# Scores of two heads issued in turn into pairs of PSUM banks, and the bias table built in the first projection

## The chip, the cores and the metric

The kernel runs on one core of a Trainium2 chip, in one launch. The metric is the device time of that launch in microseconds (us). TensorE multiplies matrices into PSUM (eight banks of 128 partitions x 512 float32), VectorE and ScalarE (ACT) read PSUM and write SBUF, GpSimd (POOL) works on SBUF and issues small loads, and SyncE (SP) issues the loads of weights.

## The reference

Two layers over 256 tokens of width 1024, all in float32. Each layer has a mixer of three attention branches that share one input projection, and a squared-ReLU MLP.

```python
h = rms_norm(x, norm_mix_pre[l])
dq, dk, dv, mq, mk, mv, c_q, c_kv, k_pe, g = split(h @ w_in[l])
# differential: 4 heads, each with two halves of 64 features
w  = softmax(q1 k1^T/8 + bias) - lam * softmax(q2 k2^T/8 + bias)
oa = rms_norm(w @ v, diff_subln[l]) * (1 - lam_init)
# block attention: 4 heads of 128; one block holds the whole sequence, so it is causal attention
ob = softmax(q k^T * 128**-0.5 + bias) @ v
# latent: 8 heads, 64 features and 32 with rotary positions; values of 64
oc = softmax(q k^T * 96**-0.5) @ v
x  = x + rms_norm(sum(sigmoid(g) * (o @ w_branch)) @ w_out, norm_mix_post[l])
x  = x + rms_norm(relu(rms_norm(x) @ w_up)**2 @ w_down, norm_mlp_post[l])
```

`bias` comes from a table of 32 buckets by 8 heads, looked up by the distance between query and key (T5 buckets); keys behind the query's place are masked.

## The kernel before

Instructions are written in program order with tiles and pools. A planner then fixes the order of each engine's instructions before the run: it takes what is ready by its own estimate of times, and of several ready ones the one that is first in program order. On the chip each engine follows that order and waits at an instruction whose inputs are late.

Weights are float32 and split exactly into two parts (`hi` by ACT at L129, `lo` by VectorE at L130); each product of a projection is three TensorE passes (L176 to L178). Weights are loaded by SP (L137), 512 KB at a time, into five buffers; the split parts have six buffers each.

A layer's mixer runs, in program order: the projection of the latents (`pc`, two token tiles); their norms (`rr`, `cr` are powers on POOL at L117; `cn`, `rope` read `pc`); values and queries and keys of the differential heads (`dv`, `dqk`); in layer 0 the bias table, `lam` and the rotary factors; the differential heads; the same for the block heads (`mv`, `mqk`); the latent heads; then gates (`pg`), the products of the branches (`pb`) and the output projection (`po`). The planner fills TensorE's time between steps of attention with `pmv`, `pmqk` and `pg` products.

A head's scores are two float32 products, 128 queries x 128 keys (L354) and 128 queries x 256 keys (L355), each of which the chip runs as two passes. `softmax` adds the bias (VectorE, L345) and takes the exponent (ACT, L348). Probabilities are transposed on TensorE (L361), copied by ACT (L363, `pt`) and multiplied with the values (L374 and L375 for block and latent heads, L500 to L502 for differential ones). A differential head uses the scores' banks again: `pss[0]` for its output, `pss[1]` for the transposed output (L516).

PSUM: the pool `p_acc` has four single banks, `p_mm` two, `p_tr` two. `p_acc` holds the scores, `pc`, `pcols` (rows of norm weights brought onto partitions), `pb`, and the accumulators of the output projection and of the MLP's second product (four at once).

The bias table is built by `setup_bias`: two small loads on POOL (`oh`, `tab`), one product (`pbias`, L266), a copy into a staging tile `cb` (L270), a write to scratch memory in HBM (L272), and a load of 1152 KB that spreads it over 128 partitions (L274). `cb`, `oh` and the tiles `cn`, `lamv`, `lamp` share the three buffers of the pool `prep`.

Of the kernel before, what the change touches and what calls it, by code (L numbers as in the profile page):

```python
# [30 lines left out]
# First relative distance of each T5 bucket that distances 0..255 can reach.  # L31
# [4 lines left out]
def trunk(ctx: ExitStack, tc: tile.TileContext, x, positions, rel_bias, norm_mix_pre, norm_mix_post,  # L36
# [15 lines left out]
    p_acc = ctx.enter_context(tc.tile_pool(name="pacc", bufs=4, space=PSUM))  # L52
# [18 lines left out]
    def acc_tile(name):  # L71
        return p_acc.tile([128, 512], F32, tag="acc", name=name)
# [11 lines left out]
    # Rows of vectors that act on features once those lie on partitions.  # L84
# [26 lines left out]
    def setup_cols(rows, at, n):  # L111
        p = acc_tile("pcols")
        nc.tensor.transpose(p[:, :n], rows[:], ident[:n, :n])
        nc.vector.tensor_copy(cols[:, at:at + n], p[:, :n])
# [17 lines left out]
    def chunk(src, nk, c, name, parts=None, spare=None, quick=False):  # L132
        """One load of weights and its two parts; `spare` is a pool that is idle now."""
        n = nk * c
        raw = raws.tile([128, 1024], F32, tag="raw", name=f"raw_{name}")
        rv = raw[:, :n].rearrange("p (k c) -> p k c", k=nk)
        nc.sync.dma_start(rv, src)  # L137
        if spare is None:
            hi = whi.tile([128, 1024], F32R, tag="hi", name=f"hi_{name}")
            lo = wlo.tile([128, 1024], F32R, tag="lo", name=f"lo_{name}")  # L140
        else:
            pool, tag = spare
            hi = pool.tile([128, 1024], F32R, tag=tag, name=f"hi_{name}")
            lo = pool.tile([128, 1024], F32R, tag=tag, name=f"lo_{name}")
        if parts is None:
            split(hi[:, :n], lo[:, :n], raw[:, :n], quick)
        else:
            at = 0
            for v in parts(raw):
                m = v.shape[1] * v.shape[2]  # L150
                o = [t[:, at:at + m].rearrange("p (a b) -> p a b", a=v.shape[1]) for t in (hi, lo)]
                split(o[0], o[1], v)
                at += m
        return [(hi[:, k * c:(k + 1) * c], lo[:, k * c:(k + 1) * c]) for k in range(nk)]
# [4 lines left out]
    def load_t(w2d, c0, c, name, kts=KT):  # L159
        """Weights that move: kts tiles of [128, c]."""  # L160
        nk = 1024 // c
        r = []
        for k0 in range(0, kts, nk):
            r += chunk(wslice(w2d, k0, nk, c0, c), nk, c, f"{name}_{k0}")
        return r

    def load_f(w2d, c0, name, kts=KT):
        """Weights that stay: two blocks of 128 columns, kts tiles each."""
        r = []
        for k0 in range(0, kts, 4):  # L170
            r += chunk(wslice(w2d, k0, 4, c0, 256), 4, 256, f"{name}_{k0}")
        return [[(h[:, b * 128:(b + 1) * 128], l[:, b * 128:(b + 1) * 128]) for h, l in r] for b in range(2)]
# [58 lines left out]
    def post_norm(xt, ps2, wpost, eps_col):  # L231
        """x += rms_norm(ps2) * wpost"""
        parts = small_tile("pnp", 2)
        yw = slab_tile([128, D], "yw")
        def weigh(h):
            nc.vector.tensor_tensor(yw[:, h * 512:(h + 1) * 512], ps2[h][:],
                                    wpost[:, h * 512:(h + 1) * 512], op=OP.mult)
        for h in range(2):
            nc.scalar.activation(junk, ps2[h][:], AF.Square, scale=1.0 / 32.0, accum_out=parts[:, h:h + 1])
            if h == 0:  # L240
                weigh(0)
        v = small_tile("pnv", 1)
        nc.vector.tensor_scalar(v, parts[:, 0:1], parts[:, 1:2], EPS if eps_col is None else eps_col,
                                op0=OP.add, op1=OP.add)
        q = small_tile("pnq", 1)
        rpow(q, v, 1)
        weigh(1)
        for h in range(2):
            s = slice(h * 512, (h + 1) * 512)
            nc.vector.scalar_tensor_tensor(xt[:, s], yw[:, s], q[:, 0:1], xt[:, s],  # L250
                                           op0=OP.mult, op1=OP.add)

# [24 lines left out]
    def setup_rope():  # L277
# [14 lines left out]
        # Index 0: sine.  Index 1: cosine, the sine a quarter turn on.  # L292
# [24 lines left out]
    def setup_lam():  # L317
# [10 lines left out]
        for l in range(DEPTH):  # L328
            li = 0.8 - 0.6 * math.exp(-0.3 * l)
            nc.vector.tensor_scalar(lam[:, l:l + 1], dots[:, 2 * l:2 * l + 1], dots[:, 2 * l + 1:2 * l + 2], li,  # L330
                                    op0=OP.subtract, op1=OP.add)
            # The weights come out of the chip negated: the sign goes here.
            nc.vector.tensor_scalar(subc[:, l:l + 1], cols[:, 38 + l:39 + l], -(1.0 - li), None, op0=OP.mult)

# [1 line left out]
    last_exp = [None]  # L336

    def softmax(ps, brow):
        e = work_tile("e", "e", 384, 6)
# [12 lines left out]
    def scores(q, k):  # L352
        ps = acc_tile("sc")
        nc.tensor.matmul(ps[:, 0:128], q[:, 0:128], k[:, 0:128], start=True, stop=True)  # L354
        nc.tensor.matmul(ps[:, 128:384], q[:, 128:256], k, start=True, stop=True)  # L355
        return ps

    def transpose_p(p):
        ps = tr_tile("ppt")
        for j in range(3):  # L360
            nc.tensor.transpose(ps[:, j * 128:(j + 1) * 128], p[:, j * 128:(j + 1) * 128], ident[:])  # L361
        pt = work_tile("pt", "pt", 384, 2)
        nc.scalar.activation(pt, ps[:, :384], AF.Copy)  # L363
        return pt
# [7 lines left out]
    def av_f(ps, pt, v0, v1):  # L372
        """ps [c, 256 queries] = v^T p^T"""
        nc.tensor.matmul(ps, v0, pt[:, 0:256], start=True, stop=False)  # L374
        nc.tensor.matmul(ps[:, 128:256], v1, pt[:, 256:384], start=False, stop=True)  # L375

# [7 lines left out]
    def mixer(l, xs, tiles, wc, before):  # L384
# [7 lines left out]
        # latent queries, keys and the shared rope key, token-major  # L392
        wc = wc or load_c(l, 0, 4)
        pcs = []
        for t in range(2):
            pc = acc_tile("pc")
# [3 lines left out]
        if l == 0:  # L400
            more_rows()
            setup_cols(rows1, 16, n_rows - 16)
        rpow(rr, ms, 2)
# [21 lines left out]
        # 1/rms of every token along the free axis, on all partitions  # L425
# [26 lines left out]
        # transposed latents  # L452
# [16 lines left out]
        if l == 0:  # L469
            setup_bias()  # L470
# [4 lines left out]
        # differential attention  # L475
        o_a = []
        for p in range(2):
            ot = out_r(f"oa{p}")
            o_a.append(ot)
            for hh in range(2):  # L480
                h = 2 * p + hh
                es, pss = [], []
                for c in range(2):
                    ps = scores(dqk[p][c * 64:(c + 1) * 64, 0, hh, :], dqk[p][c * 64:(c + 1) * 64, 1, hh, :])
                    pss.append(ps)
                    es.append(softmax(ps, h))
                (e1, s1), (e2, s2) = es
# [34 lines left out]
        # block attention: one block holds the whole sequence, so each query sees its own block  # L522
# [3 lines left out]
        for p in range(2):  # L526
            ot = out_r(f"ob{p}")
            o_b.append(ot)
            for hh in range(2):
                h = 2 * p + hh  # L530
                ps = scores(mqk[p][:, 0, hh, :], mqk[p][:, 1, hh, :])
# [4 lines left out]
                av_f(ps[:, :256], pt, mv[:, 0, vs], mv[:, 1, vs])  # L536
                split_out(ot, hh, ps)

        # latent attention
# [49 lines left out]
        for p in range(2):  # L589
# [21 lines left out]
            for hh in range(2):  # L611
                hs = []
                for par in range(2):
                    qk = lqk[p, par]
                    ps = scores(qk[0:96, 0, hh, :], qk[0:96, 1, hh, :])
                    e, sm = softmax(ps, 8)
                    normalize_p(e, sm)
                    hs.append((4 * p + 2 * hh + par, ps, e))
                po = hs[0][1]
                for par, (h, _, e) in enumerate(hs):  # L620
                    pt = transpose_p(e)
                    vs = slice(h * 64, (h + 1) * 64)
                    av_f(po[par * 64:(par + 1) * 64, :256], pt, vl[:, 0, vs], vl[:, 1, vs])
# [3 lines left out]
        # gates and the products of the three branches, two feature blocks at a time  # L627
# [15 lines left out]
        for d in range(4):  # L643
            m = None
            for b in range(3):
# [3 lines left out]
                pb = acc_tile("pb")  # L649
# [12 lines left out]
        # output projection  # L662
# [15 lines left out]
    def finish(accs, held, xs, wpost, eps_cols, nxt, wcol, stored=None):  # L678
        """The last rows of a projection, the first half of the tokens ahead, and the norm that follows."""
# [15 lines left out]
    def out_proj(l, w2d, act, wpost, xs):  # L695
        """x += rms_norm(mixed @ w_out); the next block's input follows each half of the tokens."""
        tiles = new_act("h2")
        accs = [[acc_tile(f"po{t}{h}") for h in range(2)] for t in range(2)]
# [13 lines left out]
    def mlp(l, xs, tiles, before):  # L712
# [46 lines left out]
        def down(g):  # L759
            if not accs:  # L760
                accs.extend([acc_tile(f"pd{t}{h}") for h in range(2)] for t in range(2))
# [79 lines left out]
```

## Time and profile before

| | us |
|---|---|
| runs | 873.63, 875.62, 876.04 |
| median | 875.62 |
| span of the profiled execution | 874.3 |
| TensorE busy in it | 858.1 |
| VectorE, ACT, POOL busy in it | 539.6, 468.9, 107.1 |

The span goes from the first to the last instruction of one profiled execution; this execution's whole time is not listed apart from it. Busy times overlap. TensorE's passes are pipelined, and the profile models their ends, so that the time that a pass costs is read from its start to the start of the next one. A granted clock of 1.00 is 2.4 GHz, and 0.50 is 1.2 GHz.

### The profile page before, as it was taken

How to read it: one execution, taken by the hardware profiler on the slowest of the kernel's cores; microseconds unless marked ns; L12 is line 12 of the kernel's file. 1: busy time of each engine (PE TensorE's matmuls, PEld its weight loads, DVE VectorE, ACT ScalarE, POOL GpSimd, SP SyncE). 2: the span in 40 equal slices, each digit the busy share in tenths (PEclk: the TensorE clock that was granted, in tenths of full speed). 3: DMA queues.
4: the chain of work that ended last, by engine and by line, in shares of the span. 5: the costliest groups of instructions: out<-in, count | busy, mean ns of one | idle time of the engine just before them, and what ended most of it. 6: DMA issues, size and time to landing. Idle time of an engine off the chain costs nothing.

```text
span 874.3 us, 14960 instructions
## 1 busy us (share of the span) xinstructions
PE 858.1 (98%) x5820; PEld 791.0 (90%) x5820; DVE 539.6 (62%) x921; ACT 468.9 (54%) x820; POOL 107.1 (12%) x130
## 2 busy tenths in 40 slices
PE   7999999999999999999999999999999999999997
PEld 6988999899988999999899899999998899999995
DVE  6757688457867445446575768954578754554452
ACT  6536675644546444445464757664544664444441
POOL 2211210001311000000100012000033010000010
PEclk9999999999999999999999999999999999999999
DMA  8865544356666656667738553546558466665631
GB/s 275 260 168 180 144 124 134 107 178 184 203 232 195 185 182 189 191 193 212 228 97 248 146 149 97 150 117 189 177 187 270 145 218 191 192 193 182 186 115 49
DMA packets 109798, 154.27 MB, mean 176 GB/s; under 512 B 5103, under 2 KB 89136, under 8 KB 109728
## 3 DMA queue, kind: packets, MB, share of 16 engines
q1 hardware_dynamic: 108448, 149.70, 56.4%
q10 hardware_dynamic: 608, 2.11, 0.7%
q0 software_dynamic: 672, 1.51, 0.6%
q8 instruction: 46, 0.75, 0.4%
q14 instruction: 24, 0.20, 0.1%
HBM read 151.19 MB, written 2.11 MB: 175 GB/s over the span
## 4 chain that ended last, share of the span: by engine, by line
PE 88%; issue 4%; DMA 3%; DVE 2%; ACT 1%; POOL 1%; SPq 0%; POOLq 0%; DVEq 0%; ACTq 0%
PE pu L176 7%; PE pu L178 7%; PE pu L177 7%; PE pd L177 6%; PE pd L178 6%; PE pd L176 6%; PE pg L176 5%; PE pg L177 5%; PE pg L178 5%; PE pb L178 3%; PE pb L177 3%; PE pb L176 3%; PE pmqk L178 2%; PE pmqk L177 2%; PE pmqk L176 2%
## 5 line engine op out<-in xcount | busy, mean ns | idle before, releaser
L177 PE MATMUL pu<-h,hi_up 128*128 128x256 f32 x448 | 126.9, 283 | 0.0
L178 PE MATMUL pu<-h,lo_up 128*128 128x256 f32 x448 | 126.8, 283 | 0.0
L176 PE MATMUL pu<-h,hi_up 128*128 128x256 f32 x448 | 126.7, 283 | 0.0
L130 DVE TENSOR_TENSOR lo_wd<-raw_wd,hi_wd 128x1024 fp32r<-128x1024 f32 x64 | 77.7, 1225 | 74.5 <-ACT hi_wd L129 74.5
L129 ACT ACTIVATE hi_wd<-raw_wd 128x1024 fp32r<-128x1024 f32 x64 | 67.0, 1058 | 82.6 <-PE pu L177 38.0
L176 PE MATMUL pg<-h,hi_g 128*128 128x256 f32 x384 | 110.6, 288 | 0.4 <-ACT lqk L602 0.4
L178 PE MATMUL pg<-h,lo_g 128*128 128x256 f32 x384 | 109.7, 286 | 0.0
L177 PE MATMUL pg<-h,hi_g 128*128 128x256 f32 x384 | 109.1, 284 | 0.0
L130 DVE TENSOR_TENSOR lo_up<-raw_up,hi_up 128x1024 fp32r<-128x1024 f32 x64 | 80.2, 1258 | 38.8 <-ACT hi_up L129 38.5
L129 ACT ACTIVATE hi_up<-raw_up 128x1024 fp32r<-128x1024 f32 x64 | 67.9, 1064 | 59.5 <-PE pu L177 29.0
L176 PE MATMUL pd<-hi_wd,u 128*128 128x512 f32 x256 | 99.9, 390 | 0.0
L177 PE MATMUL pd<-lo_wd,u 128*128 128x512 f32 x256 | 99.8, 390 | 0.0
L178 PE MATMUL pd<-hi_wd,u 128*128 128x512 f32 x256 | 99.6, 389 | 0.0
L176 PEld LDWEIGHTS pu<-h,hi_up 128*128 128x128 f32 x448 | 85.9, 192 | 0.6
L177 PEld LDWEIGHTS pu<-h,hi_up 128*128 128x128 f32 x448 | 85.9, 192 | 0.5
L178 PEld LDWEIGHTS pu<-h,lo_up 128*128 128x128 f32 x448 | 85.9, 192 | 0.1
L130 DVE TENSOR_TENSOR lo_g<-raw_g,hi_g 128x1024 fp32r<-128x1024 f32 x48 | 58.6, 1222 | 39.0 <-ACT hi_g L129 38.7
L176 PEld LDWEIGHTS pg<-h,hi_g 128*128 128x128 f32 x384 | 73.5, 191 | 1.4 <-ACT lqk L602 0.6
L177 PEld LDWEIGHTS pg<-h,hi_g 128*128 128x128 f32 x384 | 73.5, 191 | 0.5 <-issue 0.3
L178 PEld LDWEIGHTS pg<-h,lo_g 128*128 128x128 f32 x384 | 73.5, 191 | 0.1
L129 ACT ACTIVATE hi_g<-raw_g 128x1024 fp32r<-128x1024 f32 x48 | 50.5, 1057 | 40.2 <-PE pg L177 32.2
L752 POOL TENSOR_TENSOR r<-r 128x512 f32<-128x512 f32 x28 | 30.6, 1094 | 262.1 <-ACT u L751 230.9
(293 smaller groups left out, 2109.2 us busy)
## 6 DMA issues: line engine op xcount, KB each, us to landing
raw_up<-in_w_up_dram SPq DMA_DIRECT2D x64, 512.0 KB, 3.9
raw_wd<-in_w_down_dram SPq DMA_DIRECT2D x64, 512.0 KB, 4.2
raw_g<-in_w_in_dram SPq DMA_DIRECT2D x48, 512.0 KB, 3.8
raw_br<-in_w_branch_dram SPq DMA_DIRECT2D x24, 512.0 KB, 4.1
raw_dqk<-in_w_in_dram SPq DMA_DIRECT2D x16, 512.0 KB, 5.2
raw_mqk<-in_w_in_dram SPq DMA_DIRECT2D x16, 512.0 KB, 4.1
raw_wo<-in_w_out_dram SPq DMA_DIRECT2D x16, 512.0 KB, 3.9
raw_dv<-in_w_in_dram SPq DMA_DIRECT2D x8, 512.0 KB, 4.9
```

What stands on the lines that cost most here:

```text
L129: nc.scalar.activation(dst_hi, src, AF.Copy)
L130: nc.vector.tensor_tensor(dst_lo, src, dst_hi.bitcast(F32), op=OP.subtract)
L176: i = nc.tensor.matmul(ps, sh, mh, start=first, stop=False)
L177: nc.tensor.matmul(ps, sh, ml, start=False, stop=False)
L178: nc.tensor.matmul(ps, sl, mh, start=False, stop=last)
L752: nc.gpsimd.tensor_tensor(r, r, r, op=OP.mult)
```

## The change

The pool `p_acc` now gives pairs of banks (two, in place of four single banks). `scores2` issues the scores of two heads (for a differential head, of its two halves) in turn: first both products of 128 keys, then both of 256. For latent heads both transposes of probabilities come ahead, and the products with the values are issued in turn (`av_f`). Where one bank is needed (`pc`, `pcols`, `pb`), the other bank of the pair stays empty. `setup_bias` moves from behind the projections of `dv` and `dqk` to right behind the products of `pc`. The buffers of `e` go from six to five, those of `pt` from two to three. The rest of the diff removes comments.

```diff
-    p_acc = ctx.enter_context(tc.tile_pool(name="pacc", bufs=4, space=PSUM))
+    p_acc = ctx.enter_context(tc.tile_pool(name="pacc", bufs=2, space=PSUM))
...
-    def acc_tile(name):
-        return p_acc.tile([128, 512], F32, tag="acc", name=name)
+    def acc_pair(name):
+
+        t = p_acc.tile([128, 2, 512], F32, tag="acc", name=name)
+        return t[:, 0, :], t[:, 1, :]
...
-        p = acc_tile("pcols")
+        p, _ = acc_pair("pcols")
...
-        e = work_tile("e", "e", 384, 6)
+        e = work_tile("e", "e", 384, 5)
...
-    def scores(q, k):
-        ps = acc_tile("sc")
-        nc.tensor.matmul(ps[:, 0:128], q[:, 0:128], k[:, 0:128], start=True, stop=True)
-        nc.tensor.matmul(ps[:, 128:384], q[:, 128:256], k, start=True, stop=True)
-        return ps
+    def scores2(qks):
+
+        pss = acc_pair("sc")
+        for ps, (q, k) in zip(pss, qks):
+            nc.tensor.matmul(ps[:, 0:128], q[:, 0:128], k[:, 0:128], start=True, stop=True)
+        for ps, (q, k) in zip(pss, qks):
+            nc.tensor.matmul(ps[:, 128:384], q[:, 128:256], k, start=True, stop=True)
+        return pss
...
-        pt = work_tile("pt", "pt", 384, 2)
+        pt = work_tile("pt", "pt", 384, 3)
...
-    def av_f(ps, pt, v0, v1):
-        """ps [c, 256 queries] = v^T p^T"""
-        nc.tensor.matmul(ps, v0, pt[:, 0:256], start=True, stop=False)
-        nc.tensor.matmul(ps[:, 128:256], v1, pt[:, 256:384], start=False, stop=True)
+    def av_f(parts):
+
+        for ps, pt, v0, v1 in parts:
+            nc.tensor.matmul(ps, v0, pt[:, 0:256], start=True, stop=False)
+        for ps, pt, v0, v1 in parts:
+            nc.tensor.matmul(ps[:, 128:256], v1, pt[:, 256:384], start=False, stop=True)
...
-            pc = acc_tile("pc")
+            pc, _ = acc_pair("pc")
...
             setup_cols(rows1, 16, n_rows - 16)
+            setup_bias()
...
         if l == 0:
-            setup_bias()
             setup_lam()
...
-                es, pss = [], []
-                for c in range(2):
-                    ps = scores(dqk[p][c * 64:(c + 1) * 64, 0, hh, :], dqk[p][c * 64:(c + 1) * 64, 1, hh, :])
-                    pss.append(ps)
-                    es.append(softmax(ps, h))
-                (e1, s1), (e2, s2) = es
+                pss = scores2([[dqk[p][c * 64:(c + 1) * 64, j, hh, :] for j in range(2)] for c in range(2)])
+                (e1, s1), (e2, s2) = [softmax(ps, h) for ps in pss]
...
-            for hh in range(2):
+            pss = scores2([[mqk[p][:, j, hh, :] for j in range(2)] for hh in range(2)])
+            for hh, ps in enumerate(pss):
                 h = 2 * p + hh
-                ps = scores(mqk[p][:, 0, hh, :], mqk[p][:, 1, hh, :])
...
-                hs = []
-                for par in range(2):
-                    qk = lqk[p, par]
-                    ps = scores(qk[0:96, 0, hh, :], qk[0:96, 1, hh, :])
+                pss = scores2([[lqk[p, par][0:96, j, hh, :] for j in range(2)] for par in range(2)])
+                es = []
+                for ps in pss:
                     e, sm = softmax(ps, 8)
                     normalize_p(e, sm)
-                    hs.append((4 * p + 2 * hh + par, ps, e))
-                po = hs[0][1]
-                for par, (h, _, e) in enumerate(hs):
-                    pt = transpose_p(e)
+                    es.append(e)
+                po = pss[0]
+                parts = []
+                for par, e in enumerate(es):
+                    h = 4 * p + 2 * hh + par
                     vs = slice(h * 64, (h + 1) * 64)
-                    av_f(po[par * 64:(par + 1) * 64, :256], pt, vl[:, 0, vs], vl[:, 1, vs])
+                    parts.append((po[par * 64:(par + 1) * 64, :256], transpose_p(e), vl[:, 0, vs], vl[:, 1, vs]))
+                av_f(parts)
...
-                pb = acc_tile("pb")
+                pb, _ = acc_pair("pb")
...
-        accs = [[acc_tile(f"po{t}{h}") for h in range(2)] for t in range(2)]
+        accs = [acc_pair(f"po{t}") for t in range(2)]
...
-                accs.extend([acc_tile(f"pd{t}{h}") for h in range(2)] for t in range(2))
+                accs.extend(acc_pair(f"pd{t}") for t in range(2))
```

## Rows read from the trace of the kernel before

**Rows 1.** The page, busy times of the engines, and bytes moved in 40 slices

```profile
PE 858.1 (98%) x5820; PEld 791.0 (90%) x5820; DVE 539.6 (62%) x921; ACT 468.9 (54%) x820; POOL 107.1 (12%) x130
...
GB/s 275 260 168 180 144 124 134 107 178 184 203 232 195 185 182 189 191 193 212 228 97 248 146 149 97 150 117 189 177 187 270 145 218 191 192 193 182 186 115 49
```

**Rows 2.** Waits of TensorE: total us, times, longest us

```profile
PE ppt L361 <- DVE e L495: 2.0, 1, 2.0
...
PE ppt L361 <- DVE e L369: 0.5, 1, 0.5
```

**Rows 3.** Timeline of TensorE around 72 us: start, us, [idle before <-releaser]

```profile
71.19 0.28 PE L176 MATMUL pmqk<-h,hi_mqk 128*128 128x256 f32 x1
71.31 0.28 PE L177 MATMUL pmqk<-h,hi_mqk 128*128 128x256 f32 x1
73.57 0.33 PE L361 MATMUL ppt<-ident,e 128*128 128x128 f32 x1 [1.98 <-DVE e L495]
```

**Rows 4.** Windows: busy us by engine, granted clock, DMA share, GB/s

```profile
74.12:77.53 3.41, 3.41 (x19) 3.41 (x18) 3.34 (x7) 3.16 (x7) 0.00 (x0) 0.50 0.88 253
```

**Rows 5.** Timeline of POOL, 20 to 64 us

```profile
23.23 3.09 POOL L117 TENSOR_TENSOR cr<-cv,halves 128x2 f32<-128x2 f32 x2
...
57.10 0.53 POOL L272 DMA_DIRECT2D scr<-cb  x1
62.94 1.04 POOL L274 DMA_DIRECT2D bias<-scr  x1 [5.32 <-DMA scr<-cb]
```

**Rows 6.** Timeline of VectorE, 57 to 70 us

```profile
62.78 0.43 DVE L324 TENSOR_TENSOR lamp<-lamv 128x256 f32<-128x256 f32 x1 [3.79 <-DMA scr<-cb]
...
69.35 0.29 DVE L345 CUSTOM_DVE_ANT_0 e<-sc,bias 128x128 f32<-128x128 f32 x1 [3.09 <-DMA bias<-scr]
```

**Rows 7.** Timeline of TensorE, four places of the first layer

```profile
25.77 0.38 PE L428 MATMUL prb<-ident,rr 128*128 128x128 f32 x2
...
55.02 0.59 PE L266 MATMUL pbias<-oh,tab 32*8 32x256 f32 x2
...
203.29 0.28 PE L176 MATMUL pb<-oa,hi_br 128*128 128x256 f32 x1
...
237.85 0.40 PE L176 MATMUL po<-hi_wo,mixed 128*128 128x512 f32 x1
```

**Rows 8.** Loads: issuing queue, count, KB each, us from issue to landing

```profile
bias<-scr POOLq DMA_DIRECT2D x1, 1152.0 KB, 6.4
```

**Rows 9.** Timeline of TensorE, scores of differential heads in the first layer

```profile
56.02 0.50 PE L354 MATMUL sc<-dqk 64*128 64x128 f32 x4
...
56.78 0.49 PE L354 MATMUL sc<-dqk 64*128 64x128 f32 x4
...
57.64 0.50 PE L176 MATMUL pmv<-hi_mv,h 128*128 128x512 f32 x1
...
85.70 0.48 PE L354 MATMUL sc<-dqk 64*128 64x128 f32 x2
...
86.55 0.39 PE L178 MATMUL pmqk<-h,lo_mqk 128*128 128x256 f32 x1
```

**Rows 10.** Timeline of TensorE, products of latent heads with their values

```profile
149.48 0.65 PE L374 MATMUL sc<-pt,vl 128*64 128x256 f32 x2
...
150.27 0.55 PE L361 MATMUL ppt<-ident,e 128*128 128x128 f32 x3
...
159.87 0.66 PE L374 MATMUL sc<-pt,vl 128*64 128x256 f32 x4
...
160.68 0.55 PE L361 MATMUL ppt<-ident,e 128*128 128x128 f32 x3
```

**Rows 11.** Timeline of VectorE, end of attention and of the branches' products

```profile
170.07 0.42 DVE L670 TENSOR_TENSOR oc<-sc,oc 128x256 fp32r<-128x256 f32 x1
...
237.81 0.68 DVE L653 TENSOR_TENSOR br<-pb,g 128x512 f32<-128x512 f32 x1
...
239.54 0.69 DVE L653 TENSOR_TENSOR br<-pb,g 128x512 f32<-128x512 f32 x1
```

More of the change, by code (lines that the diff above doesn't have):

```diff
@@ L535, in mixer @@
                 vs = slice(h * 128, (h + 1) * 128)
-                av_f(ps[:, :256], pt, mv[:, 0, vs], mv[:, 1, vs])
+                av_f([(ps[:, :256], pt, mv[:, 0, vs], mv[:, 1, vs])])
                 split_out(ot, hh, ps)
```

## The prediction, on record before the changed kernel ran

> **What bounds the kernel now.** I read the page first: TensorE has work in 98% of the span, and the other engines have idle time throughout [rows 1]. Time can then only be won where TensorE takes longer from one start to the next than the work needs, or waits. So I went to the list of what TensorE waited for. Beside the input loads of the first 8 us it holds two entries that bear on the change: one wait of 2.0 us for the differential heads' probabilities and one of 0.5 us for the block heads' [rows 2]. Third, the timeline around the first: the product that starts at 71.31 is followed by the next only at 73.57, where 0.12 us is usual (71.19 to 71.31), so 2.14 us are lost [rows 3]. Fourth, the windows of that stretch: right after the wait TensorE's granted clock is 0.50, its 1.2 GHz level, from 74.12 to 77.53 us [rows 4]. A product takes about twice its time there, so half of 3.41 us, 1.7 us, is lost as well. The wait costs 2.14 + 1.7 = 3.8 us; I keep 3.7, as part of the transposes there would not have been faster. Fifth, who was late: the bias table. Its two loads leave POOL at 57.10 (to scratch) and 62.94 (back, spread), and the second is issued after 5.32 us of waiting for the first [rows 5]. VectorE stands at the head weights `lamp` until 62.78, for the scratch write that still reads the staging tile `cb`, and then 3.09 us more until 69.35 for the table itself [rows 6]. Its softmax steps stand behind that, and TensorE's transposes behind those. The second layer, which has the table, shows no such wait: the entry counts one [rows 2].
>
> **The change, part by part.**
>
> *Bias table earlier.* Moved: two small loads, one pair of TensorE passes, two memsets and a copy, the scratch write and the read back. The passes cost the same at either place: 0.59 us with their overlap [rows 7]. What they gain is the wait and the clock: -3.7 us. Bounds: 0, if the table still comes behind the projections; -3.8, if nothing else is late next. Next in line are the splits of `mqk` weights and the softmax steps themselves, which in the second layer come without a wait [rows 2]; so I take nearly the whole.
>
> The read back moves 1152 KB, 1.18 MB [rows 8], now among the weight loads of some 20 to 40 us. At the 253 GB/s that the busiest window shows [rows 4] that is 4.7 us of the transfer engines. Cover: a 512 KB load of weights feeds 24 products of 0.12 us [rows 3], 2.9 us, so TensorE needs about 182 GB/s; the second slice of the page moved 260 for 21.9 us [rows 1], 1.7 MB ahead of need. I cost the load at 0; without that cover it is up to 4.7 us.
>
> *POOL's and TensorE's queues.* The table's steps now stand on POOL with the powers of the first projection (`rr`, then `cr` twice, 3.09 us from 23.23) [rows 5], whose results ACT and VectorE need to empty `pc`. Each `pc` now takes a pair, so both pairs are taken, and the transpose of the second set of rows (`pcols`) has to wait on TensorE until one `pc` is emptied. Before, it had a bank of its own. Lower bound 0: TensorE's transpose of `rr` stands at 25.77 [rows 7], although `rr` was ready when `cr` began at 23.23 [rows 5], so the plan puts such steps late enough. Upper bound: the read back, waiting for the scratch write, is planned ahead of both `cr`; that is worked out as a rival, 7.4 us. I take 1.0 us, between the two waits of 0.5 and 2.0 that differ from plan in [rows 2].
>
> *Scores of two heads in turn, differential.* The two halves of a head use rows 0 to 63 and 64 to 127 of the array. Where both halves are issued in turn, the whole head takes 56.02 to 56.78, 0.76 us; the next such head 56.78 to 57.64, 0.86. A half by itself takes 85.70 to 86.55, 0.85 [rows 9], thus 1.70 for a head. In each layer the first two heads are in turn and the last two are not (eight single halves, at 85.7, 87.7, 90.4, 94.3 and 507.9, 509.4, 512.7, 514.2), because their two banks come free one after the other. A pair of banks comes free at once, so all four remaining heads go in turn: 4 x (1.70 - 0.81) = -3.6 us. Bounds: 0 to -3.8. The Trainium skill (TensorEngine Tiling (Array Packing), Key Properties) says that changing the tiling mode drains TensorE; if the planner put one full-array product between the four instructions of each head, as it does between the output transposes, I estimate from that rule two more drains per head, and the gain would be some 2 us instead of 3.6. All ten groups of 64-row scores in the trace stand without such a product between them, so I stay with 3.6.
>
> *Scores of block and latent heads in turn.* They use all or 96 of the rows, and before they already follow each other without a gap where four are ready. 0, both ways; the cover is not needed.
>
> *Products with the values of two latent heads in turn.* These write columns 0 to 63 and 64 to 127. A single one takes 149.48 to 150.27, 0.79 us; two in turn 159.87 to 160.68, 0.81 [rows 10]. Four of the eight pairs are in turn already (159.9, 567.1, 571.3, 575.6). If the other four join them: 4 x (1.58 - 0.81) = -3.1 us. But the planner issues whatever is ready, and the second head's transposed probabilities come later than the first's; if none joins the gain is 0, and if the four that are in turn fall apart it is +3.1. With both transposes now ahead of both products I take half of it, -1.5.
>
> *Pairs in place of single banks elsewhere.* `pb` uses one bank of a pair, so two are in flight and not four. A product block lasts 24 x 0.12 = 2.9 us, and one emptying 0.68; in the trace only the last `pb` but one of a layer is emptied later than a block after its end. The output projection begins at 237.85 [rows 7] and its first accumulators would wait for the emptying of the last `pb` but one, 237.81 + 0.68 = 238.49 [rows 11]: 0.65 us, and the same in layer two, +1.3 us. Bounds 0 (if VectorE is planned otherwise) and +2.0 (if the second pair, free at 240.2, is late too by about 0.35).
>
> *Pair hand-overs in attention.* A pair comes free only when both its heads are done. The chain gets longer, but it ends at about 170.5 us [rows 11] and its first reader `pb` starts at 203.29 [rows 7], 33 us later, with gate products filling in. Only plan errors cost: +0.5 us, one wait like the 0.5 [rows 2]. Bounds 0 and the rival below. One `e` buffer fewer and one `pt` more: 0, since at most four `e` live at once in two heads; if a fifth were needed it would be one more such wait.
>
> Sum: -3.7 - 3.6 - 1.5 + 1.0 + 1.3 + 0.5 = -6.0 us. The profiled span is 874.3 us, 1.3 below the median of 875.62, and what lies around it is not touched; so 868.3 in the span and 869.6 for the median.
>
> **The rivals.**
> *No change: POOL's queue in the first projection.* If the table's TensorE passes run at about 21 us, the scratch write leaves at some 22 and is read back at 27.8 at the earliest (57.10 to 62.94 is 5.84), plus 1.04 us of issue [rows 5]. If the plan has that issue ahead of both `cr`, they end at 28.9 + 3.1 = 32.0 in place of 26.3, 5.7 us late; ACT, `pc` and so TensorE at `pcols` wait that long, and a wait like that brings the half clock again, 1.7 more: 7.4. Sum: -8.8 + 1.8 + 7.4 = +0.4, 876.0 us. For it: in the profile the engines stood behind precisely this pair of loads [rows 6]. Against: the plan need only put the read back behind `cr`, and nothing asks for `pcols` early.
>
> *Slower: hand-overs of pairs.* Each layer uses ten pairs in attention, eight of them handed over, sixteen in all. If TensorE waits 0.6 us at each, for the slower head's last reader, that is 9.6 us; -8.8 + 1.0 + 1.3 + 9.6 = +3.1, 878.7 us. It decides from 0.57 us at each, where the sum passes +2.6. For it: a wait of 0.5 at just such a place [rows 2]. Against: that is one in two layers, and gate products stand ready. The Trainium skill (TensorEngine Tiling (Array Packing), PSUM Bottleneck) says that tiling speeds TensorE but not the emptying of PSUM, which is this mechanism; no row before shows the pairs.
>
> *The table stays late.* If the planner still places the table's passes behind the projections, -3.7 and its +1.0 fall away: -3.3, 872.3 us. Against: the passes now rank above these projections in program order, and their load needs only a free staging tile.
>
> *Everything joins.* All latent pairs in turn and no new wait: -10.4, 865.2 us.
>
> **How the numbers follow.** Forecast (-3 to -9): 0.51. Everything joins: 0.08. Table late: 0.10. POOL's queue, no change: 0.18. Hand-overs, slower: 0.13. A change under 0.3%, 2.6 us, can't be told from none here. Faster: 0.51 + 0.08 + 0.10 and a little of the no-change case, 0.70; same 0.17; slower 0.13. The range runs from all gains without costs, 865.2, to the no-change case: 865.2 to 876.0, which leaves out the slower rival and some tails.
>
> **What would show it.** Right: no wait of TensorE for L495's successor in the first layer, and a granted clock of 1.00 from 13 us to the end; all eight differential heads at 0.76 to 0.86 us; value products of latent heads in groups of four. Wrong: a TensorE wait at `pcols` or near 30 us with a half clock behind it; many waits of half a microsecond at the first score of a pair; a gap of more than 0.7 us ahead of `po`.

## The result: slower, by two costs that the sum did not hold and one with the wrong sign

The changed kernel takes 880.0 us (879.41 to 880.93, four runs) against 875.12 us for the kernel before beside it: a ratio of 1.0062, 95% interval 1.0047 to 1.0076. The forecast was 869.6 us and its range ended at 876.0; the result lies outside it and on the other side of no change. The profiled span is 877.8 us against 874.3.

The page of the kernel after, busy times and granted clock in 40 slices, answers to [rows 1]: TensorE is as full as before.

```profile
PE 856.5 (98%) x5820; PEld 786.7 (90%) x5820; DVE 539.7 (61%) x921; ACT 468.1 (53%) x820; POOL 105.5 (12%) x130
...
PEclk9999999999999999999999999999999999999998
```

The waits of TensorE after (total us, times, longest) answer to [rows 2]. Both waits for `e` are gone; the waits for `lqk`, `x`, `br` and that of `pc` for `h` are new or longer. That of `pu` for `h` stood before as well (1.2).

```profile
PE pg L178 <- ACT lqk L605: 2.8, 2, 1.4
PE pin L203 <- DVE x L252: 1.5, 3, 0.6
PE po L178 <- DVE br L657: 1.1, 2, 0.6
PE pu L178 <- DVE h L213: 1.1, 2, 0.5
PE pc L178 <- DVE h L213: 0.7, 1, 0.7
```

POOL's timeline after (start, us, idle before) answers to [rows 5] and shows why the table is early: the scratch write leaves at 25.20 in place of 57.10, between the two `cr`, and the read back stands behind both of them. The window below it (columns as in [rows 4]) holds the stretch where the half clock was: 1.00 throughout.

```profile
23.32 1.92 POOL L119 TENSOR_TENSOR cr<-cv,halves 128x2 f32<-128x2 f32 x1
25.20 0.57 POOL L274 DMA_DIRECT2D scr<-cb  x1
25.79 0.91 POOL L119 TENSOR_TENSOR cr<-cv,halves 128x2 f32<-128x2 f32 x1
30.33 1.07 POOL L276 DMA_DIRECT2D bias<-scr  x1 [3.63 <-DMA scr<-cb]
```

```profile
65.00:80.00 15.00, 15.00 (x114) 14.23 (x113) 9.72 (x14) 9.80 (x19) 1.77 (x4) 1.00 0.48 140
```

TensorE's timeline after, later differential heads, answers to the single halves of [rows 9]. Two heads stand in one group of sixteen instructions, 0.76 us from the first head's start to the second's.

```profile
82.59 0.49 PE L358 MATMUL sc<-dqk 64*128 64x128 f32 x4
82.91 0.60 PE L360 MATMUL sc<-dqk 64*128 64x256 f32 x4
83.35 0.39 PE L358 MATMUL sc<-dqk 64*128 64x128 f32 x4
83.57 0.60 PE L360 MATMUL sc<-dqk 64*128 64x256 f32 x4
```

The latent products after, same view, answer to [rows 10]. The first head's two passes of L380 go alone (149.48 to 150.05), and gate products (left out here) stand before the rest follows at 151.36.

```profile
149.48 0.65 PE L380 MATMUL sc<-pt,vl 128*64 128x256 f32 x2
150.05 0.55 PE L366 MATMUL ppt<-ident,e 128*128 128x128 f32 x3
...
151.36 0.43 PE L380 MATMUL sc<-pt,vl 128*64 128x256 f32 x1
151.37 0.43 PE L382 MATMUL sc<-pt,vl 128*64 128x128 f32 x2
151.63 0.38 PE L380 MATMUL sc<-pt,vl 128*64 128x256 f32 x1
151.84 0.38 PE L382 MATMUL sc<-pt,vl 128*64 128x128 f32 x2
152.16 0.55 PE L366 MATMUL ppt<-ident,e 128*128 128x128 f32 x3
```

**Where the time went.** The list of waits holds only idle time. To see all of it I took, for each TensorE instruction of a profile, the time from its start to the start of the next, and summed by the tile written; a wait is thus booked to the instruction ahead of it. "Outside" is what lies ahead of the first start and behind the last. The columns e1 to e9 are the experiments below (e3 is left out). `pin` are the transposes that bring the input of a block, a norm's result, into the layout of the next products; `pkn` are the latent keys, `pu` and `pd` the two products of the MLP.

```
tile           before  after     e1     e2     e4     e5     e6     e7     e8     e9
sc<-dqk          10.0    6.2    6.2    9.0    9.2    6.2    9.0    6.2    6.4    6.2
pmqk             52.6   48.0   48.0   48.8   48.8   48.0   48.8   48.0   50.0   48.0
ppt, pg         152.4  151.7  151.7  152.7  151.7  151.0  151.7  151.6  153.1  151.3
sc<-pt,vl         9.6   11.0   11.0   11.0    8.0    9.6    8.0   11.0   11.0    9.6
pkn               3.3    6.5    6.5    3.4    3.4    6.5    3.4    4.7    4.7    4.7
pb               69.1   71.0   70.8   69.1   69.1   70.6   69.1   71.2   70.4   71.3
pin              11.4   13.4   12.1   11.9   11.6   11.5   12.3   11.5   13.5   11.5
po               43.8   45.3   44.0   43.8   43.8   44.0   43.8   44.0   45.3   44.0
pd              174.3  175.1  174.3  174.3  174.3  174.3  174.3  174.3  175.1  174.3
pc               21.2   21.0   20.0   20.9   20.2   21.5   20.4   19.6   22.2   22.0
all others      316.8  317.4  317.5  317.3  317.3  317.5  317.4  317.7  316.9  317.3
first to last   864.4  866.5  862.0  862.2  857.5  860.6  858.2  859.7  868.5  860.1
outside           9.9   11.3    9.7   10.1   10.1    9.8   10.1    9.9   11.4    9.8
span            874.3  877.8  871.7  872.3  867.6  870.4  868.3  869.6  879.9  869.9
```

Before to after, the wanted gains are there: -3.8 at the differential scores, -4.6 at `pmqk` (what of it is the table's, e4 and e8 show). Against them stand +3.2 behind `pkn`, +1.9 at `pb`, +1.4 at the latent products, and +2.1, +1.5, +0.7 and +1.4 at `pin`, `po`, `pd` and outside, 5.7 together, nearly all at the norms behind the output and the down projection (`pin` also holds the waits for the first input, 0.3 of the 2.1).

The row `pc` needs care. Its part in the second layer is 9.0 or 9.1 us in every profile; its part in the first layer goes from 10.5 (e7) to 13.1 (e8), by two things that none of the edits aims at. One is a wait for the second load of `x`, 0.1 to 1.1 us, which is booked there. The other is where TensorE's granted clock first reaches 1.00: in e8, TensorE's timeline, passes of `pc` start 0.35 us apart up to 15.34 us and 0.19 from there on; in e7 the step comes at 10.22. Five passes stand ahead of it in e7, fourteen in e8.

```profile
14.65 0.55 PE L180 MATMUL pc<-hi_c,h 128*128 128x416 f32 x1
15.00 0.50 PE L181 MATMUL pc<-lo_c,h 128*128 128x416 f32 x1
15.34 0.35 PE L180 MATMUL pc<-hi_c,h 128*128 128x416 f32 x1
15.53 0.35 PE L182 MATMUL pc<-hi_c,h 128*128 128x416 f32 x1
```

So up to 2.5 us between two of these spans lie in the start of those executions, and the rows are compared one by one below.

What the norms lost is plainest at the very end. ACT's and VectorE's timelines there, first of the kernel before, with TensorE's last product:

```profile
867.69 0.39 PE L178 MATMUL pd<-hi_wd,u 128*128 128x512 f32 x1
```

```profile
864.78 0.60 ACT L239 ACTIVATE junk<-pd 128x512 bf16<-128x512 f32 x1 [2.71 <-PE pd L178]
...
868.18 0.60 ACT L239 ACTIVATE junk<-pd 128x512 bf16<-128x512 f32 x1 [2.71 <-PE pd L178]
```

```profile
865.50 0.69 DVE L236 TENSOR_TENSOR yw<-pd,wpost 128x512 f32<-128x512 f32 x1 [1.05 <-ACT junk L239]
868.90 0.27 DVE L243 TENSOR_SCALAR pnv<-pnp,ep 128x1 f32<-128x1 f32 x1 [2.71 <-ACT junk L239]
```

and of the kernel after, likewise:

```profile
869.66 0.39 PE L180 MATMUL pd<-hi_wd,u 128*128 128x512 f32 x1
```

```profile
870.14 0.60 ACT L241 ACTIVATE junk<-pd 128x512 bf16<-128x512 f32 x1 [4.72 <-PE pd L180]
...
871.59 0.60 ACT L241 ACTIVATE junk<-pd 128x512 bf16<-128x512 f32 x1 [0.76 <-DVE yw L238]
```

```profile
870.87 0.69 DVE L238 TENSOR_TENSOR yw<-pd,wpost 128x512 f32<-128x512 f32 x1 [3.06 <-ACT junk L241]
872.31 0.27 DVE L245 TENSOR_SCALAR pnv<-pnp,ep 128x1 f32<-128x1 f32 x1 [0.76 <-ACT junk L241]
```

`junk` is the square of a half row, `yw` its product with the norm's weights, `pnv` the sum of both halves' squares. Before, the first half of the row was squared and weighed (864.78, 865.50) while TensorE still worked on the second half. After, that square comes only behind the last product of the second half, and the second square waits for the first half's `yw`: from the last product's start to `pnv` it is 2.65 us (872.31 - 869.66) in place of 1.21 (868.90 - 867.69).

### The profile page after: what moved, and what is told of

It reads as the page before. It is cut to its first block, busy times and chain, and to the rows that moved or that the text cites. A ratio compares the mean times of both kernels' runs of the same rounds, so it can differ in the third digit from the quotient of the medians.

```text
span 877.8 us, 14927 instructions
## 1 busy us (share of the span) xinstructions
PE 856.5 (98%) x5820; PEld 786.7 (90%) x5820; DVE 539.7 (61%) x921; ACT 468.1 (53%) x820; POOL 105.5 (12%) x130
## 4 chain that ended last, share of the span: by engine, by line
PE 93%; issue 2%; ACT 2%; DVE 1%; POOL 1%; DMA 1%; SPq 0%; DVEq 0%; POOLq 0%; ACTq 0%
PE pu L178 7%; PE pu L180 7%; PE pu L179 7%; PE pd L179 6%; PE pd L178 6%; PE pd L180 6%; PE pg L178 5%; PE pg L180 5%; PE pg L179 5%; PE pb L179 2%; PE pb L178 2%; PE pb L180 2%; PE pmqk L179 2%; PE pmqk L178 2%; PE pdqk L180 2%
```

## Experiments

Each was timed beside the kernel before (875.52 us for e1 to e4, 874.91 for e5 to e8, 874.05 for e9). As its time differs by 1.5 us between these three comparisons, experiments of different ones are best set against each other by their ratios.

**e1: accumulators crossed.** Pair h now holds half h of both token tiles, in place of both halves of one.

```diff
-        accs = [acc_pair(f"po{t}") for t in range(2)]
+        accs = list(zip(*[acc_pair(f"po{h}") for h in range(2)]))
...
-                accs.extend(acc_pair(f"pd{t}") for t in range(2))
+                accs.extend(zip(*[acc_pair(f"pd{h}") for h in range(2)]))
```

> The changed kernel (880.0 us), with the accumulators of the output projection and of the MLP's second product crossed: one pair holds the first column half of both token tiles, the other pair the second half. Theory A: a pair is one tile to the framework's tracking of dependences, so that the norm which follows could not read one bank until the products of the other bank had ended, four times in the kernel; crossed, a token tile's two halves lie in different tiles, and the 1.0 + 1.95 + 1.0 us that TensorE lost behind these norms and the 1.4 us at the end come back: about 5.4 us less, 874.6 us, and the last square of a norm starts within 1 us of its own products' end. Rival B: tracking is by bank, and the loss comes from pairs coming free late: nothing comes back, 879 to 882 us.

874.21 us, ratio 0.9990 (0.9979 to 1.0001): 5.8 us come back. The wait of `pin` for `x` is gone from TensorE's list, and the first half's square (ACT's timeline) stands again ahead of the last product, which starts at 865.12:

```profile
862.19 0.60 ACT L241 ACTIVATE junk<-pd 128x512 bf16<-128x512 f32 x1 [2.70 <-issue]
...
865.59 0.60 ACT L241 ACTIVATE junk<-pd 128x512 bf16<-128x512 f32 x1 [2.71 <-issue]
```

The number of banks, pairs and products is the same; only which halves share a pair differs. In the table `pin`, `po`, `pd` and outside give back 5.0 and `pc` 1.0. The part of `pin` ahead of the first layer is 0.4 longer, by its wait for the input. Without that part and the time ahead of TensorE's first start, and with the second layer's `pc` (0.1), the norms cost 5.7 us and 5.5 come back. The other 0.9 at `pc` is in the first layer, where the wait for the second load of `x` is 0.1 in place of 1.0 us, and has nothing to do with the norms. So the loss is that of two halves sharing a pair, and it is shown.

**e2: four single banks,** with the order of issue and the early table of the change.

```diff
-    p_acc = ctx.enter_context(tc.tile_pool(name="pacc", bufs=2, space=PSUM))
+    p_acc = ctx.enter_context(tc.tile_pool(name="pacc", bufs=4, space=PSUM))
...
-        t = p_acc.tile([128, 2, 512], F32, tag="acc", name=name)
-        return t[:, 0, :], t[:, 1, :]
+        return [acc_tile(f"{name}{i}") for i in range(2)]
```

> The changed kernel with four single banks in place of two pairs everywhere; the order of issue in turn, the early table and all else stay. Theory A: the 5.4 us of the norms and 1.4 us ahead of the output projection come back, and the third and fourth differential head of a layer fall apart into single halves again, which costs 3.6 us: about 877 us, or 874 if the two waits of 1.45 us for ACT at the first gate product go with the pairs as well. Rival C: issue in turn in program order is enough to keep the halves of a head together: all eight heads at 0.76 to 0.86 us, and 871 to 873 us.

873.96 us, ratio 0.9979 (0.9967 to 0.9991). The three losses of the pairs vanish in the table (`pkn` 3.4, `pb` 69.1, norms as before), and so does most of the scores' gain (9.0): the third and fourth head fall apart as theory A had it, but for one in the first layer, and rival C falls. The program's order of the scores alone brings little: e4, which lacks it, has 9.2. The latent products stay at 11.0.

**e3: table's steps back in their old place,** the rest as changed.

```diff
-            setup_bias()
...
         if l == 0:
+            setup_bias()
```

> The changed kernel with the bias table built where it was before, behind the projections of the differential heads. If the early table is worth what the prediction said, the wait of some 2 us for the first transposes of probabilities and the half clock behind it come back: 3.7 us more, 883.7 us. Rival: the first layer's gain of 4.5 us came from the pairs, and the table is hidden either way: 880 us.

880.55 us, ratio 1.0057 (1.0038 to 1.0076): no difference, and not the 883.7 expected. TensorE's timeline says why:

```profile
31.45 0.59 PE L268 MATMUL pbias<-oh,tab 32*8 32x256 f32 x2 [0.68 <-DMA oh<-in_onehot_dram]
31.97 0.39 PE L178 MATMUL pdqk<-h,hi_dqk 128*128 128x256 f32 x1
```

The planner moved the table's passes ahead of the `dqk` products by itself, to 31.45, where the kernel before has them at 55.02 [rows 7]. The run thus says nothing about a late table; e8 does.

**e4: the kernel before with the table early and nothing else.**

```diff
             setup_cols(rows1, 16, n_rows - 16)
+            setup_bias()
...
-            setup_bias()
```

> The kernel before with only the bias table moved to the first projection. If the early table is worth what the prediction said: 3.7 us less than the kernel before, 871.4 us, with no granted clock of 0.50 between 13 us and the end of the products. Rival: the table's steps on POOL hold up the first projection: 875 us or more.

869.65 us, ratio 0.9936 (0.9917 to 0.9955), the fastest of all. `pmqk` falls by 3.8, as the prediction had it; the plan that goes with the early table orders the rest of the first layer better too: one more differential head in turn (-0.8) and two more latent pairs, six of eight (-1.6; 6 x 0.81 + 2 x 1.58 = 8.0). TensorE's timeline shows two of those, all four products of two heads in one group although the program issues head by head:

```profile
134.33 0.66 PE L374 MATMUL sc<-pt,vl 128*64 128x256 f32 x4
134.81 0.40 PE L375 MATMUL sc<-pt,vl 128*64 128x128 f32 x4
...
138.63 0.66 PE L374 MATMUL sc<-pt,vl 128*64 128x256 f32 x4
139.12 0.40 PE L375 MATMUL sc<-pt,vl 128*64 128x128 f32 x4
```

The 1.0 less at `pc` is all in the first layer: the wait for `x` is 0.7 shorter, and the clock reached 1.00 at 11.03 us in place of 12.68.

**e5 and e6: latent products head by head again,** on e1 and on e2.

```diff
-                    parts.append((po[par * 64:(par + 1) * 64, :256], transpose_p(e), vl[:, 0, vs], vl[:, 1, vs]))
-                av_f(parts)
+                    av_f([(po[par * 64:(par + 1) * 64, :256], transpose_p(e), vl[:, 0, vs], vl[:, 1, vs])])
```

> The crossed kernel (874.2 us) with one part of the change undone: each latent head's two products with the values are issued right behind its own transposes again, head by head, and not both heads' in turn by the program. Theory: the joint order is what breaks the pairing, because the first head's first product is issued alone as soon as its probabilities are there and only the three others overlap (1.37 us a pair, 10.97 us in all eight). Head by head the planner brings two heads' four products together, as it does in the kernel before with the table early (8.03 us), so 874.2 - 2.9 = 871.3 us, at least 872.8 if only half of the pairs join (9.6 us). Rival: the pairing is set by when the probabilities arrive, which the pair of score banks fixes, so the order in the program changes nothing: 874.2 us.

> The kernel with four single banks (873.96 us) with the same part undone: latent products head by head. What then is left of the change is the early table, the scores in turn in single banks, and the numbers of e and pt buffers. Theory: the joint order of the products costs 2.94 us there (10.97 against 8.03 us), so 871.0 us; if the 0.75 us more at the transposes of the probabilities are due to it too, 870.3 us. Rival: the loss against the kernel before with the table early (869.65 us) comes from the scores in turn or from the buffers of e and pt, so 874 us.

e5: 873.03 us, ratio 0.9979 (0.9965 to 0.9992), 1.2 us less than e1 (1.0 by the ratios, whose intervals overlap, so that it is the table that shows the gain), and 9.6 in the table: the lesser of the two gains expected. e6: 870.45 us, ratio 0.9950 (0.9938 to 0.9962), 3.5 us less than e2 (2.5 by the ratios), with 8.0 and 1.0 less at `ppt, pg`. The order that the program asks for does break the pairing: with both heads' first products ahead of both heads' second ones, the first head's product still goes as soon as its transposes are there, and leaves three of the four to overlap (8 x 1.37 = 11.0). With pairs only four of the eight join, so the rival is right in part: the pairs matter as well. That they do so by when the probabilities arrive is argued and was not tried apart.

e6 differs from e4 only in the scores in turn and in the numbers of `e` and `pt` buffers. Their intervals overlap, and no row of the table differs by more than 0.2 but `pin`, by 0.7, all of it waiting for the first input. So neither of the two costs or brings anything that can be seen in single banks.

**e7: copies of the latent queries on VectorE,** on e1.

```diff
-                nc.scalar.activation(lqk[g, par][0:64, 0], qv, AF.Copy, scale=sc)
+                nc.vector.tensor_scalar(lqk[g, par][0:64, 0], qv, sc, None, op0=OP.mult)
```

> The crossed kernel (874.2 us) with the copies of the latent queries out of PSUM moved from ACT to VectorE. Theory: in each layer the first gate product waits 1.4 us because ACT has two splits of gate weights ahead of these copies (108.12 to 110.03 us, copies from 110.03), while VectorE stands idle for 1.02 us just then; on VectorE the copies come at once and 2 x 1.2 us go: 871.8 us. Rival: the wait is one of two banks that are written by two projections and emptied by whatever engine; VectorE has the keys' copies to do there already (0.69 us each), so the same wait returns there at 1 us or more: 873.5 to 874.5 us.

872.25 us, ratio 0.9973 (0.9961 to 0.9985): 2.0 of the 2.4 us against e1 (1.5 by the ratios, whose intervals just overlap; `pkn` falls by 1.8). In the kernel after, ACT's timeline at this place has two splits of gate weights ahead of the copies:

```profile
108.12 2.01 ACT L131 ACTIVATE hi_g<-raw_g 128x1024 fp32r<-128x1024 f32 x2 [0.51 <-PE pqn L179]
110.03 1.18 ACT L605 ACTIVATE lqk<-pqn 64x512 f32<-64x512 f32 x2
```

and TensorE's next product waits for them, 1.39 us after the last of `pkn`:

```profile
111.26 0.38 PE L178 MATMUL pg<-h,hi_g 128*128 128x256 f32 x1 [1.39 <-ACT lqk L605]
```

With the copies on VectorE the list of waits has, for both layers together:

```profile
PE pg L178 <- DVE lqk L605: 1.0, 2, 0.5
```

So most of the wait, 1.8 of 2.8 us, is for the copy's place in ACT's queue; 0.5 in each layer is left with VectorE's copies. With ACT's copies it is 1.4 in both layers of the kernel after, of e1, e3 and e5, and in the second layer of e8, and 0.4 at most with single banks; why the plan with pairs puts the splits first was not tried.

**e8: table really late.** As e3, and its first TensorE pass ordered behind the last `dqk` product (`last_mm` is set in `mm3`).

```diff
-        nc.tensor.matmul(p[:8, :256], tab[:], oh[:], start=True, stop=True)
+        order_after(nc.tensor.matmul(p[:8, :256], tab[:], oh[:], start=True, stop=True), last_mm[0])
```

> The changed kernel (880.0 us) with the bias table's steps in their old place, and its pair of TensorE passes held behind the last product of the differential queries and keys, so that the plan can't move it up as it did without that. Theory: the wait for the table (2.1 us) and the half clock behind it (1.7 us) return: 883.7 us, with a stretch of granted clock 0.50 near 74 us and a wait of TensorE of about 2 us for the differential heads' probabilities. Rival: with pairs the plan of this stretch differs so far from the kernel before that the table's lateness is covered by other products, or costs the wait alone: 880 to 882 us.

880.95 us, ratio 1.0067 (1.0052 to 1.0082): the rival's side. The wait returns, as TensorE's timeline shows (72.62 to 74.52, 1.8 us longer than usual), but the window around it keeps a granted clock of 1.00:

```profile
72.62 0.28 PE L181 MATMUL pmqk<-h,hi_mqk 128*128 128x256 f32 x1
74.52 0.33 PE L368 MATMUL ppt<-ident,e 128*128 128x128 f32 x1 [1.62 <-DVE e L500]
```

```profile
72.00:80.00 8.00, 6.38 (x55) 6.17 (x54) 7.86 (x19) 8.00 (x19) 0.68 (x3) 1.00 0.48 127
```

In the table `pmqk` rises by 2.0. `pkn` falls by 1.8, but most of that is only booked elsewhere: the first layer's wait now stands behind another product, within `ppt, pg`, which rises by 1.4. TensorE's list of waits has for it:

```profile
PE pg L180 <- ACT lqk L607: 1.4, 1, 1.4
PE pg L180 <- DVE lqk L608: 1.0, 1, 1.0
```

The 1.2 more at `pc` is in the first layer as well, nearly all by the clock's rise, at 15.32 us in place of 12.45. The end comes out 1 us above the kernel after, and the ratios' intervals overlap, so a late table costs less than 3.7 us in a kernel with pairs; the two plans differ in more than the lines that were edited.

**e9: the three mended together** (e1, the edit of e5, the edit of e7).

> All three mended together: accumulators crossed, latent products head by head, copies of the latent queries on VectorE. What is left of the pairs is their gain at the differential heads' scores. If the single edits add up: 874.2 - 1.2 - 2.0 = 871.0 us, ratio 0.9950, still behind the kernel before with the early table alone (869.65 us, ratio 0.9936): then the pairs aren't worth having even without these three losses, for pb to po (about 1.7 us) and latent products that join in half of the cases (9.6 against 8.0 us) take what the scores give. Rival: with the waits gone the plan brings the latent products together as well, 871.0 - 1.6 = 869.4 us, and pairs and single banks stand level.

871.02 us, ratio 0.9961 (0.9948 to 0.9975). The single edits add up, in time and in the ratios too (e1's 0.9990 less 0.0011 of e5 and 0.0017 of e7 is 0.9962; the 0.9950 expected mixed the times of different comparisons), and the latent products stay at 9.6, so the rival falls. Against e4 the pairs bring 3.0 us at the differential scores and 0.8 at `pmqk`, and cost 2.2 at `pb`, 1.6 at the latent products and 1.3 behind `pkn`; a further 1.8 at `pc` is all in the first layer, where the wait for `x` is 0.5 longer and the clock reached 1.00 at 14.96 us, in e4 at 11.03. The intervals of e4 and e9 overlap (up to 0.9955 and from 0.9948), so that the times don't tell the mended pairs from the table alone; the rows, without `pc`, have the pairs slightly behind.

## Why the prediction was wrong, point by point

**The step that failed** is "Pairs in place of single banks elsewhere". It asked only who waits for a pair when it changes hands, at `pb` to `po`. There it was about right: +1.3 was forecast and `pb` rose by 1.9, of which 1.4 at the step from its last product to the first of `po` (0.84 us in each layer, 0.12 before). It never asked what happens while a pair is held: `po` and `pd` hold the two halves of a row, which ACT and VectorE read one after the other while TensorE fills the second. The rows stood in the trace of before (the square at 864.78 ahead of the last product at 867.69), but none of [rows 1 to 11] is of a norm. That is 5.7 us in the table, and 5.5 of them came back in e1, whose time fell by 5.8: by itself nearly the whole predicted gain.

**Latent products in turn:** -1.5 was forecast between -3.1 and +3.1, and +1.4 came. The bound was right, the middle of it was not a finding: the sentence that "the second head's transposed probabilities come later than the first's" already described what happened. e6 puts the price of the edit at 2.5 to 3.5 us in single banks (3.0 at the latent products), e5 at 1.0 to 1.2 with pairs (1.4 there).

**Pair hand-overs:** +0.5 was forecast. No wait stands at the first score of a pair, so the slower rival's sixteen waits did not come, though its end did (878.7 by it). What came is one wait of 1.4 us per layer behind `pkn`, +3.2 in the table, for a copy on ACT; a plan error such as the +0.5 was meant for, but more than twice its size and in both layers.

**Differential scores:** -3.6 forecast, -3.8 measured, eight heads of eight in turn; that it takes the pairs is shown by e2 (9.0 of the 10.0 us). The estimate from the drain rule of the Trainium skill (TensorEngine Tiling (Array Packing), Key Properties), some 2 us, does not apply here: no other product was planned into these groups. The drain's price in it came from no row, and no run here shows one. Nor does a run test what the same page says of emptying (PSUM Bottleneck), that tiling speeds TensorE and not what empties PSUM: most of what was lost does stand at readers of PSUM (5.7 at the norms, 3.2 at `lqk`, 1.9 at `br`), but e1 and e7 trace the first to halves that share a pair and most of the second to an order on ACT, not to faster scores.

**Table early:** -3.7 forecast; `pmqk` fell by 4.6 with the pairs and by 3.8 without (e4), and the half clock of [rows 4] is gone in both. In e4 only the table moved, and its 3.8 bear the forecast out; the rest of its 5.9 us is the better order behind. With the pairs the near hit is in part luck: by e8 the table's place is worth 2.0 of the 4.6 there, and the other 2.6 came with the plan of the pairs, in which not even a late table brought the half clock.

**POOL's and TensorE's queues:** +1.0 forecast, about 0 measured (`pc` -0.2). The rival in which the read back stands ahead of both `cr` fell: it stands behind them.

The sum: -6.0 forecast for the span, +3.5 measured. The norms account for +5.7 of the 9.5 between them, the latent products for 2.9, the wait behind `pkn` for 2.7 beyond the 0.5, `pb` for 0.6; the queues (-1.2), the table (-0.9) and the scores (-0.2) came out better, and -0.1 lies in small terms.

## What to carry to other kernels

A tile over two PSUM banks is one thing to wait for: before joining banks, list every reader that starts on one while the other is being written, above all in epilogues that work half by half, and pair those banks that finish far apart (e1: 5.8 us for two lines of pairing). An order of issue written into the program is a request that the planner fills with whatever is ready; if the parts come ready at different times, the order can split a group that it was meant to make. And a bundle of edits should be run apart: here one part of it was worth 5.9 us alone, and the bundle lost 4.9.

## What the runs showed of the hardware

An idle time of TensorE of 1.62 us in the first layer (e8) left the granted clock at 1.00, and so did the 1.39 us behind `pkn` in the kernel after; the one of 1.98 us in the kernel before [rows 3] was followed by 3.41 us at 0.50 [rows 4]. I had expected the half clock behind e8's wait as well. What decides between them was not tried.

In the eleven profiles the granted clock first reached 1.00 between 10.23 us (e7) and 15.32 us (e8), with TensorE's first instruction at 3.07 to 3.31 us in each. By the rows of `pc` the passes ahead of that start 0.35 us apart and those behind it 0.19; nine more of them stood ahead of it in e8 than in e7, which makes an estimated 9 x 0.16 = 1.4 us between the two that no edit asked for.
